# Mean squares of the second attention's norm: one float32 matmul, or two float32r matmuls of the squares' high and low parts

## The chip, the cores and the metric

The kernel runs on one core of a Trainium2 chip. A core has a matrix engine (TensorE, PE), whose weight loads have a column of their own in the profile (PEld), a vector engine (VectorE, DVE), a scalar engine (ScalarE, ACT), a general engine (GpSimd, POOL) and an engine that issues most transfers (SyncE, SP). Each engine works through its own list of instructions in order, and semaphores between the lists hold an instruction until its operands are there. The metric is the device time of one execution in microseconds (us), less is better; the times given are medians of several runs.

## The reference

The program is a trunk of two layers on 1024 rows of 1024 float32 values. Layer 0 mixes tokens by latent attention, layer 1 by differential attention; each mixer is followed by its output projection, a layer norm with the residual, a SwiGLU feed-forward part (2816 wide) and another layer norm. The change is in the mixer of layer 1 alone. Cut to it:

```python
def _rmsnorm(x, g):
    y = x32 * lax.rsqrt(jnp.mean(jnp.square(x32), axis=-1, keepdims=True) + RMS_EPS)
    return (y * g.astype(jnp.float32)).astype(x.dtype)

def _diff_mixer(x, w_in, ..., g_sub, w_o, lambda_init):
    q, k, v = jnp.split(x @ w_in, ...)        # 8 heads, 2 maps of 64, values of 128
    ...                                       # for each block of 128 query rows:
        p = jax.nn.softmax(logits, axis=-1)   # scores * scale - slope * distance, chunk mask
        a = p[:, 0] - lam * p[:, 1]
        o = jnp.einsum('bhqk,bkhe->bqhe', a.astype(v.dtype), v, ...)
    o = _rmsnorm(o, g_sub) * (1.0 - lambda_init)    # over the 128 values of a head
    return o.reshape(b, s, DIFF_HEADS * DIFF_V) @ w_o
```

For every head and row the norm needs the mean of 128 squares.

## The kernel before, in words

Products of float32 matrices are made of three matmuls of type float32r: each operand is split into a high part (a cast to float32r) and a low part (what the cast left off), and high x high, high x low and low x high are summed in PSUM. The helper `split` (L486, L487) makes the parts, with the cast on ACT and the subtraction on another engine, most often DVE. Only a few matmuls take float32 operands as they are; the one for the mean squares is among them.

The second attention runs from about 1135 to 1575 us. `attention` goes through pairs (head h, block i of 128 query rows), eight blocks to a head; the last head goes in the order 6, 7, 4, 5, 2, 3, 0, 1. For each pair there are three steps, with the scores two blocks ahead of the transposes:

- `score_b`: for both softmax maps the scores go into a PSUM bank `s_b` (matmuls, L228). DVE adds the bias, moves them into an SBUF tile `l_b` and takes the extreme of each row (L231). ACT makes the exponential in place (L234), POOL scales the second map (L1306) and DVE joins the two (L1307).
- `turn_b`: TensorE transposes the joined map into PSUM `pt_b` (L160); ACT casts it to the high part `pth_b` (L255), DVE subtracts the low part `ptl_b` (L256).
- `mix_b`: for a group g of two blocks, TensorE multiplies by the values (`o_b`, L267), and DVE copies the result into `bo`, which has the 128 values of the head on the partitions and the query rows along the columns (L1316).

Between these, numbered slots hold other work: `proj_b` makes queries and keys of the next head (PSUM `bp`, L155 to L157, three float32r matmuls per term), `values_b` the values (`bv`). `norm_b` and `norm_b2` of head h stand at the slots 8h+9 and 8h+10, in the next head's run. `norm_b` squares `bo` on ACT into `sq`. `norm_b2` multiplies by `ones` (a 128 x 128 matrix of 1/128) on TensorE into an `s` bank `ms`, so that each column's mean stands on all partitions. Then ACT takes logarithm (L1340) and exponential with -0.5 (L1342), and POOL multiplies `bo` by the result (L1343). Heads 0 to 5 are then written out to DRAM (L1346). Heads 0 to 6 are normed in two parts of 512 columns; the last head in groups: `sq7_3` and `sq7_2` of 256 columns, `sq7_0` of 512. Of 17 such parts 15 have 512 columns.

`l_b` and `sq` come from one ring, tag "l" of pool `lp`, with five buffers of 4 KB per partition. PSUM has three `s` banks.

In the last head `begin_out` frees the memory of `xT` (the input of `proj_b`), loads the output weights `wo` there (L358), and the rows of heads 0 to 5 come back as `of_a` (L371). The output projection splits rows into `oh_a` (ACT L394, DVE L395) and multiplies by `wo` (`zp_a`, L406).

The order of each engine's list is set by a scheduler that runs over the program with a simulated timeline when the kernel is built, and by priorities for some steps. A shorter or longer instruction thus can move others.

Of the kernel before, what the change touches and what calls it, by code (L numbers as in the profile page):

```python
# [9 lines left out]
F32 = mybir.dt.float32  # L10
F32R = mybir.dt.float32r
# [5 lines left out]
P = 128  # L17
S = 1024
# [24 lines left out]
def trunk(  # L43
# [33 lines left out]
    V, A, G, T = nc.vector, nc.scalar, nc.gpsimd, nc.tensor  # L77

    cp = ctx.enter_context(tc.tile_pool(name="cp", bufs=1))
    sp = ctx.enter_context(tc.tile_pool(name="sp", bufs=8))  # L80

    ident = cp.tile([P, P], F32, tag="ident", name="ident")
    ones = cp.tile([P, P], F32, tag="ones", name="ones")
    cst = cp.tile([P, 48], F32, tag="cst", name="cst")
    edge = ctx.enter_context(tc.tile_pool(name="edge", bufs=1, side="right"))
    late = edge.tile([P, 504], F32, tag="edge", name="edge")
    wp = ctx.enter_context(tc.tile_pool(name="wp", bufs=3))
    big = ctx.enter_context(tc.tile_pool(name="big", bufs=5))
    ps, ps_bufs, ps_stack = None, None, None
# [10 lines left out]
    dr = ctx.enter_context(tc.tile_pool(name="dr", bufs=1, space=DRAM))  # L100

    V.memset(ones, 1.0 / P)
    mhalf = cst[:, 0:2]
    V.memset(mhalf, -0.5)
    eps_rms = cst[:, 8:9]
# [2 lines left out]
    def f32(t):  # L108
        return t.bitcast(F32)
# [4 lines left out]
    def ps_s(name):  # L114
        return ps.tile([P, 512], F32, tag="s", bufs=ps_bufs[0], name=name)
# [225 lines left out]
    class OutProj:  # L341
# [50 lines left out]
        def split(self, tb, hs, o):  # L392
            oh, ol = (t[:, hs] for t in self.oh[tb])
            A.activation(oh, o, AF.Copy, scale=self.scale)  # L394
            V.scalar_tensor_tensor(ol, o, self.scale, f32(oh), ALU.mult, ALU.subtract)  # L395
# [674 lines left out]
    with ast as st:  # L1070
        pool = st.enter_context(tc.tile_pool(name="a1", bufs=2, reuse_waits="tile"))
        vp = st.enter_context(tc.tile_pool(name="a1v", bufs=12, side="right", reuse_waits="tile"))
        lp = st.enter_context(tc.tile_pool(name="a1l", bufs=4, side="right", reuse_waits="tile"))
# [155 lines left out]
    with ExitStack() as st:  # L1229
        lp = st.enter_context(tc.tile_pool(name="b1l", bufs=5, reuse_waits="tile"))  # L1230
# [4 lines left out]
        vt, lt, pts, sqs, q_slot = {}, {}, {}, {}, {}  # L1235
# [82 lines left out]
        def o_rows(h, g, n=1):  # L1318

            return ob[:, h % 2, g * 256:(g + n) * 256]  # L1320
# [4 lines left out]
        def norm_b(h, g0=0, g1=4):  # L1325

            t = lp.tile([P, S], F32, tag="l", name=f"sq{h}_{g0}")
            sqs[h, g0] = [(t[:, (g - g0) * 256:min(g + 2, g1) * 256 - g0 * 256],
                           o_rows(h, g, min(2, g1 - g))) for g in range(g0, g1, 2)]
            for sq, o in sqs[h, g0]:  # L1330
                A.activation(sq, o, AF.Square)

        def norm_b2(h, g0=0, g1=4):
            parts = []
            for i, (sq, o) in enumerate(sqs.pop((h, g0))):
                m = ps_s(f"ms{h}_{g0}_{i}")[:, :sq.shape[1]]
                T.matmul(m, ones, sq, start=True, stop=True)
                parts.append((sq, o, m))
            for r, _, m in parts:
                A.activation(r, m, AF.Ln, bias=eps_rms, scale=1.0)  # L1340
            for r, o, _ in parts:
                A.activation(r, r, AF.Exp, scale=-0.5)  # L1342
                G.tensor_tensor(o, o, r, ALU.mult)  # L1343
            if h < H - 2:
                for g in range(g0, g1):
                    nc.sync.dma_start(o_dr[1][g][h], o_rows(h, g))  # L1346
# [36 lines left out]
        for h in range(H - 1):  # L1383
            at(8 * h + 9, norm_b, h)
            at(8 * h + 10, norm_b2, h)
        at(8 * H - 6, norm_b, H - 1, 3, 4)
        at(8 * H - 5, norm_b2, H - 1, 3, 4)
        at(8 * H - 4, norm_b, H - 1, 2, 3)
        at(8 * H - 3, norm_b2, H - 1, 2, 3)

        first, second = LAST_ORDER[:2]
# [111 lines left out]
```

## Time and profile before

| | |
|---|---|
| median of 3 runs | 2294.41 us (2293.27 to 2299.95) |
| the profiled execution | 2294.99 us, its span 2293.2 us, mean granted TensorE clock 0.996 |
| PE, matmuls | 2251.4 us busy, 98% of the span |
| PEld, weight loads | 1918.7 us, 84% |
| DVE | 1560.4 us, 68% |
| ACT | 1018.6 us, 44% |
| POOL | 877.9 us, 38% |
| DMA | 289.33 MB, 126 GB/s |

The busy time of an engine is the time in which at least one of its instructions runs; an instruction's own duration can overlap that of the next, so on TensorE the distance between the starts of successive matmuls tells what each occupies. A row of the timeline has start, duration, engine, line, operation, output<-inputs, shape, count, and in brackets the wait ahead of it with the instruction that ended it. Shares are averages over stages with different limits; the row of a stretch of time tells the limit in that stretch.

### The profile page before, as it was taken

What the parts mean: (1) busy time and instruction counts of PE and PEld (TensorE: products, weight loads), DVE (VectorE), ACT (ScalarE), POOL (GpSimd) and SP (SyncE); (2) the same over time, 40 slices, a digit from 0 to 9 for tenths busy, and PEclk for the clock granted to TensorE, in tenths of its full rate; (3) what the DMA queues carried; (4) which work ended last, traced back from release to release, by engine and by line L of the source; (5) the groups of instructions that cost most, each with busy time, mean ns of one, the idle gap of its engine ahead of it and who ended that gap; (6) DMA issues with size and microseconds to landing.
All of it is one profiled execution on the core that took longest, in us unless ns stands there. A gap on an engine that the chain in (4) does not pass through costs nothing. (4 is left out here: it accounts for less than half of the span.)

```text
span 2293.2 us, 31159 instructions
## 1 busy us (share of the span) xinstructions
PE 2251.4 (98%) x11426; PEld 1918.7 (84%) x11426; DVE 1560.4 (68%) x2887; ACT 1018.6 (44%) x2101; POOL 877.9 (38%) x682
## 2 busy tenths in 40 slices
PE   9999999999999999999999999999999999999997
PEld 9888998888888887888888898977778888887886
DVE  6666665596656558777476766676587566658877
ACT  4465664342332324345455655555442233324353
POOL 2233451124444445555332424211024444436564
PEclk9999999999999999999999999999999999999999
DMA  5121335334323237544311202143344232337453
GB/s 205 41 94 61 117 99 190 142 139 144 108 87 120 93 116 305 200 176 166 104 45 33 69 25 70 38 193 120 124 166 155 70 128 80 127 126 301 144 203 123
DMA packets 104281, 289.33 MB, mean 126 GB/s; under 512 B 8640, under 2 KB 31808, under 8 KB 93632
## 3 DMA queue, kind: packets, MB, share of 16 engines
q1 hardware_dynamic: 100128, 277.90, 34.5%
q0 software_dynamic: 4000, 9.44, 1.4%
q8 instruction: 90, 1.47, 0.3%
q14 instruction: 63, 0.52, 0.1%
HBM read 205.78 MB, written 77.33 MB: 123 GB/s over the span
## 5 line engine op out<-in xcount | busy, mean ns | idle before, releaser
L486 ACT CAST op_g<-gr 128x512 fp32r<-128x512 f32 x240 | 147.5, 622 | 410.8 <-PE gb L531 229.9
L487 POOL TENSOR_TENSOR op_g<-gr,op_g 128x512 fp32r<-128x512 f32 x104 | 145.3, 1402 | 304.1 <-DVE tmp L622 154.0
L487 DVE TENSOR_TENSOR op_h<-rh,op_h 128x512 fp32r<-128x512 f32 x154 | 166.4, 1112 | 68.1 <-ACT op_h L486 68.1
L531 PE MATMUL ga<-xh_m,op_g 128*128 128x512 f32 x512 | 168.1, 389 | 0.0
L486 ACT CAST op_h<-rh 128x512 fp32r<-128x512 f32 x154 | 92.6, 619 | 148.7 <-DMA rh<-h_dr 39.9
L799 PE MATMUL dw<-op_w_t,op_h 128*128 128x512 f32 x660 | 151.5, 390 | 0.3 <-DVE op_h L487 0.3
L799 PEld LDWEIGHTS dw<-op_w_t,op_h 128*128 128x128 f32 x660 | 123.5, 188 | 26.4 <-DVE op_h L487 1.0
L234 ACT ACTIVATE l_b<-l_b,mx_b 128x256 f32<-128x256 f32 (+7 forms) x128 | 99.5, 778 | 75.9 <-DVE mx_b L231 74.0
L1306 POOL TENSOR_SCALAR l_b<-l_b,r_b,cst 128x128 f32<-128x128 f32 (+3 forms) x64 | 52.5, 821 | 207.6 <-DVE r_b L236 201.6
L487 POOL TENSOR_TENSOR op_w_t<-tt,op_w_t 128x512 fp32r<-128x512 f32 x66 | 100.1, 1521 | 80.0 <-ACT op_w_t L486 77.6
L799 PE MATMUL dx<-op_w_b,op_h 128*128 128x512 f32 x528 | 123.5, 394 | 5.4 <-ACT op_w_b L486 3.9
L799 PEld LDWEIGHTS dx<-op_w_b,op_h 128*128 128x128 f32 x528 | 99.8, 190 | 28.7 <-ACT op_w_b L486 4.7
L531 PE MATMUL gb<-t4h_f,op_g 128*128 128x512 f32 x352 | 115.9, 390 | 3.0 <-DVE tmp L614 3.0
L531 PE MATMUL gc<-b22h_f,op_g 128*128 128x512 f32 x352 | 115.6, 389 | 2.3 <-ACT op_g L486 2.3
L531 PE MATMUL gc<-t1h_f,op_g 128*128 128x512 f32 x352 | 115.5, 389 | 0.0
L487 DVE TENSOR_TENSOR op_g<-gr,op_g 128x512 fp32r<-128x512 f32 x136 | 109.5, 806 | 8.8 <-ACT op_g L486 8.2
L531 PE MATMUL gb<-t3h_f,op_g 128*128 128x512 f32 x352 | 115.2, 389 | 0.0
L531 PE MATMUL gb<-t2h_f,op_g 128*128 128x512 f32 x352 | 114.9, 389 | 0.0
L531 PEld LDWEIGHTS ga<-xh_m,op_g 128*128 128x128 f32 x512 | 96.1, 188 | 19.9
L487 POOL TENSOR_TENSOR op_g<-s,op_g 128x512 fp32r<-128x512 f32 x40 | 55.5, 1387 | 144.0 <-ACT op_g L486 144.0
L155 PE MATMUL bp<-xT_f,h_wb 128*128 128x512 f32 x256 | 102.8, 402 | 0.0
L157 PE MATMUL bp<-xT_f,l_wb 128*128 128x512 f32 x256 | 101.6, 397 | 0.0
(373 smaller groups left out, 6767.7 us busy)
## 6 DMA issues: line engine op xcount, KB each, us to landing
gr<-in_w_gu SPq DMA_DIRECT2D x44, 1024.0 KB, 6.8
rh<-h_dr SPq DMA_DIRECT2D x28, 1024.0 KB, 5.2
h_dr<-sh SPq DMA_DIRECT2D x22, 1024.0 KB, 4.9
h_dr<-hp SPq DMA_DIRECT2D x22, 768.0 KB, 4.1
tt<-in_w_dn SPq DMA_DIRECT2D x22, 512.0 KB, 7.6
rh<-h_dr SPq DMA_DIRECT2D x14, 768.0 KB, 4.4
z<-xs_dr SPq DMA_DIRECT2D x16, 512.0 KB, 11.1
rw_b<-in_w_dn SPq DMA_DIRECT2D x8, 1024.0 KB, 8.2
```

The lines of the kernel that those rows point to most:

```text
L155: T.matmul(ps_out, lh, rh, start=(i == 0), stop=False)
L157: T.matmul(ps_out, ll, rh, start=False, stop=(i == n - 1))
L234: newest["exp"] = A.activation(l[:, :n], l[:, :n], AF.Exp, bias=mx, scale=-1.0, accum_out=sm).ins
L486: A.copy(hi, src)
L487: eng.tensor_tensor(lo, src, f32(hi), ALU.subtract)
L531: T.matmul(o, w[:, a, kc], x[b][:, k, :], start=(first and k == 0 and (a, b) == (0, 0)), stop=(k == 3 and a == 1), skip_group_check=True,)
L799: T.matmul(o, h[:, a, c], w[:, b_], start=(first and (a, b_) == (0, 0)), stop=(last and a == 1), skip_group_check=True,)
L1306: G.tensor_scalar(l1[:, :n], l1[:, :n], r1, nlam, ALU.mult, ALU.mult)
```

## The change

`norm_b` splits each part's squares with `split`, the cast on ACT and the subtraction on DVE, into a tile `sp` of the ring "l", which holds the high and the low half. `norm_b2` then makes two float32r matmuls with `ones_r`, a float32r copy of `ones` made once at the start, which sum into the same bank. 1/128 is a power of two, so `ones_r` holds it in full. Room for `ones_r` comes from a tile `late` at the edge of SBUF, which becomes 128 columns narrower. The branch under `if False` isn't taken. Lines below the first edits move by 2, those below `norm_b` by 11.

```diff
--- before.py
+++ after.py
@@ -83,7 +83,8 @@
     ones = cp.tile([P, P], F32, tag="ones", name="ones")
     cst = cp.tile([P, 48], F32, tag="cst", name="cst")
     edge = ctx.enter_context(tc.tile_pool(name="edge", bufs=1, side="right"))
-    late = edge.tile([P, 504], F32, tag="edge", name="edge")
+    late = edge.tile([P, 376], F32, tag="edge", name="edge")
+    ones_r = edge.tile([P, P], F32R, tag="ones_r", name="ones_r")
     wp = ctx.enter_context(tc.tile_pool(name="wp", bufs=3))
     big = ctx.enter_context(tc.tile_pool(name="big", bufs=5))
     ps, ps_bufs, ps_stack = None, None, None
@@ -100,6 +101,7 @@
     dr = ctx.enter_context(tc.tile_pool(name="dr", bufs=1, space=DRAM))
 
     V.memset(ones, 1.0 / P)
+    A.copy(ones_r, ones)
     mhalf = cst[:, 0:2]
     V.memset(mhalf, -0.5)
     eps_rms = cst[:, 8:9]
@@ -1327,14 +1329,23 @@
             t = lp.tile([P, S], F32, tag="l", name=f"sq{h}_{g0}")
             sqs[h, g0] = [(t[:, (g - g0) * 256:min(g + 2, g1) * 256 - g0 * 256],
                            o_rows(h, g, min(2, g1 - g))) for g in range(g0, g1, 2)]
-            for sq, o in sqs[h, g0]:
+            for i, (sq, o) in enumerate(sqs[h, g0]):
                 A.activation(sq, o, AF.Square)
+                nm = f"sp{h}_{g0}_{i}"
+                if False:
+                    u = wp.tile([P, 2, 512], F32R, tag="wr", name=nm, bufs=2)
+                else:
+                    u = lp.tile([P, S], F32R, tag="l", name=nm).rearrange("p (a c) -> p a c", a=2)
+                u = [u[:, j, :sq.shape[1]] for j in range(2)]
+                split(u, sq, V)
+                sqs[h, g0][i] = (sq, o, u)
 
         def norm_b2(h, g0=0, g1=4):
             parts = []
-            for i, (sq, o) in enumerate(sqs.pop((h, g0))):
+            for i, (sq, o, u) in enumerate(sqs.pop((h, g0))):
                 m = ps_s(f"ms{h}_{g0}_{i}")[:, :sq.shape[1]]
-                T.matmul(m, ones, sq, start=True, stop=True)
+                for j in range(2):
+                    T.matmul(m, ones_r, u[j], start=(j == 0), stop=(j == 1))
                 parts.append((sq, o, m))
             for r, _, m in parts:
                 A.activation(r, m, AF.Ln, bias=eps_rms, scale=1.0)
```

In heads 0 to 6 TensorE's neighbours of the matmuls stay. Here are head 1's in TensorE's list, between the terms of a projection (`bp`, with `xT` and weights `h_wb`, `l_wb`) and the next scores (`s_b`), before:

```order
L156 MATMUL bp3_0_0_12061<-xT10_f0_10049,h_wb3_0_12057 128x512
L157 MATMUL bp3_0_0_12061<-xT00_f0_10048,l_wb3_0_12058 128x512
L1337 MATMUL ms1_0_0_12092<-sq1_0_11971,ones_62 128x512
L1337 MATMUL ms1_0_1_12094<-sq1_0_11971,ones_62 128x512
L155 MATMUL bp3_0_1_12147<-xT01_f0_10050,h_wb3_0_12057 128x512
L228 MATMUL s_b2_5_0_0_12107<-bk0_10189,bq1_10188 128x384
```

and after:

```order
L158 MATMUL bp3_0_0_12077<-xT10_f0_10051,h_wb3_0_12073 128x512
L159 MATMUL bp3_0_0_12077<-xT00_f0_10050,l_wb3_0_12074 128x512
L1348 MATMUL ms1_0_0_12108<-sp1_0_0_11983,ones_r_68 128x512 x2
L1348 MATMUL ms1_0_1_12111<-sp1_0_1_11987,ones_r_68 128x512 x2
L157 MATMUL bp3_0_1_12165<-xT01_f0_10052,h_wb3_0_12073 128x512
L230 MATMUL s_b2_5_0_0_12125<-bk0_10191,bq1_10190 128x384
```

Each of the two matmuls became two with another operand; the neighbours stayed.

In the last head, the order changes. TensorE's list around `ms7_3`, the mean squares of group 3 (rows of blocks 6 and 7), before (`zp_a` is the output projection, `pt_b` a transposed map):

```order
L228 MATMUL s_b7_3_1_0_15468<-bk1_10190,bq0_10187 128x512
L1337 MATMUL ms7_3_0_15493<-sq7_3_15441,ones_62 128x256
L228 MATMUL s_b7_3_1_0_15468<-bk1_10190,bq1_10188 128x512
L406 MATMUL zp_a1_7_1_0_15564<-wo1_5_15142,oh_a1_7_15126 128x512
L228 MATMUL s_b7_0_0_0_15519<-bk1_10190,bq0_10187 128x128
L228 MATMUL s_b7_0_0_0_15519<-bk1_10190,bq1_10188 128x128
L267 MATMUL o_b7_2_15498<-pth_b7_4_0_15417,bvh3_0_13933 128x256
```

and after:

```order
L162 MATMUL pt_b7_2_0_15602<-ident_61,l_b7_2_0_15446 128x128 x3
L1348 MATMUL ms7_3_0_15554<-sp7_3_0_15501,ones_r_68 128x256
L230 MATMUL s_b7_0_0_0_15581<-bk1_10192,bq0_10189 128x128
L230 MATMUL s_b7_0_0_0_15581<-bk1_10192,bq1_10190 128x128
L269 MATMUL o_b7_2_15560<-pth_b7_4_1_15477,bvh3_2_14453 128x256
L1348 MATMUL ms7_3_0_15554<-sp7_3_0_15501,ones_r_68 128x256
```

The matmul for `sq7_3` stood inside the second score pair of block 3; now its two halves stand behind three transposes of block 2, with two scores of block 0 and a value product between them. The score pair of `s_b7_3_1` and `zp_a` have moved ahead of six more value products (`o_b7_2`), which end just ahead of the transposes.

ACT's list at the same place, before (`L1340` and `L1342` are logarithm and exponential of the norm, `L234` the exponential of scores):

```order
L234 ACTIVATE l_b7_3_0_15457,sm_b7_3_0_15463<-l_b7_3_0_15457,mx_b7_3_0_0_15461 128x512
L1340 ACTIVATE sq7_3_15441<-ms7_3_0_15493,cst_63 128x256
L255 CAST pth_b7_4_1_15421<-pt_b7_5_0_15479 128x2x128
L1342 ACTIVATE sq7_3_15441<-sq7_3_15441 128x256
L234 ACTIVATE l_b7_3_1_15467,sm_b7_3_1_15473<-l_b7_3_1_15467,mx_b7_3_1_0_15471 128x512
L255 CAST pth_b7_2_0_15544<-pt_b7_2_0_15540 128x2x128
```

and after:

```order
L236 ACTIVATE l_b7_3_0_15518,sm_b7_3_0_15524<-l_b7_3_0_15518,mx_b7_3_0_0_15522 128x512
L257 CAST pth_b7_2_0_15606<-pt_b7_2_0_15602 128x2x128
L1351 ACTIVATE sq7_3_15499<-ms7_3_0_15554,cst_63 128x256
L1353 ACTIVATE sq7_3_15499<-sq7_3_15499 128x256
L236 ACTIVATE l_b7_3_1_15528,sm_b7_3_1_15534<-l_b7_3_1_15528,mx_b7_3_1_0_15532 128x512
L257 CAST pth_b7_2_1_15610<-pt_b7_2_0_15602 128x128
```

Logarithm and exponential of `sq7_3` stand ahead of the exponential of `l_b7_3_1` in both; the cast of `pth_b7_4_1`, which stood between the two, went ahead of all these rows, and that of `pth_b7_2_0` (L255, now L257) now stands ahead of them instead of behind.

DVE's list at the end of the last head, before (`z_a` is the residual, L414 adds the projection to it):

```order
L236 RECIPROCAL r_b7_1_1_15592<-sm_b7_1_1_15590 128x1
L414 SCALAR_TENSOR_TENSOR z_a1_6_15121,sum_a1_6_15123<-z_a1_6_15121,zp_a1_6_0_6_15657 128x512
L414 SCALAR_TENSOR_TENSOR z_a1_6_15121,sum_a1_6_15123<-z_a1_6_15121,zp_a1_6_1_6_15665 128x512
L1316 COPY bo_10191<-o_b7_1_15630 128x256
L395 SCALAR_TENSOR_TENSOR oh_a1_4_15773<-bo_10191,cst_63,oh_a1_4_15773 128x256
L1307 SCALAR_TENSOR_TENSOR l_b7_1_0_15574<-l_b7_1_0_15574,r_b7_1_0_15582,l_b7_1_1_15584 128x256
L395 SCALAR_TENSOR_TENSOR oh_a1_5_15864<-bo_10191,cst_63,oh_a1_5_15864 128x256
```

and after, in two pieces. The first stands some rows earlier, where before the list went from L231 of `l_b7_1_0` straight to L256:

```order
L233 ISA l_b7_1_0_15639,mx_b7_1_0_0_15643<-s_b7_1_0_0_15640,bb_10187 128x256
L233 ISA mx_b7_1_0_0_15643 128x1
L489 TENSOR_TENSOR sp7_2_0_15616<-sq7_2_15614,sp7_2_0_15616 128x256
L258 TENSOR_TENSOR ptl_b7_2_0_15607<-pt_b7_3_0_15661,pth_b7_2_0_15606 128x2x128
L1309 SCALAR_TENSOR_TENSOR l_b7_0_0_15580<-l_b7_0_0_15580,r_b7_0_0_15588,l_b7_0_1_15590 128x128
```

The second answers to the rows shown of before:

```order
L238 RECIPROCAL r_b7_1_1_15657<-sm_b7_1_1_15655 128x1
L416 SCALAR_TENSOR_TENSOR z_a1_6_15171,sum_a1_6_15173<-z_a1_6_15171,zp_a1_6_0_6_15723 128x512
L416 SCALAR_TENSOR_TENSOR z_a1_6_15171,sum_a1_6_15173<-z_a1_6_15171,zp_a1_6_1_6_15731 128x512
L1318 COPY bo_10193<-o_b7_1_15696 128x256
L258 TENSOR_TENSOR ptl_b7_0_0_15713<-pt_b7_0_0_15710,pth_b7_0_0_15712 128x128
L1309 SCALAR_TENSOR_TENSOR l_b7_1_0_15639<-l_b7_1_0_15639,r_b7_1_0_15647,l_b7_1_1_15649 128x256
```

The new subtraction for `sp7_2` stands ahead of the scores `l_b7_1_1`, and the split of `oh_a1_4` (L395, now L397) no longer stands ahead of the joining of `l_b7_1_0` (L1307, now L1309).

## The prediction

> **What bounds the kernel now.** I read the page's busy shares first, then busy time by stretch over the second attention (1135 to 1575 us, the only part the change touches), then the new tiles' relatives, the waits of TensorE there, and last the timeline around single places.
>
> ```profile
> PE 2251.4 (98%) x11426; PEld 1918.7 (84%) x11426; DVE 1560.4 (68%) x2887; ACT 1018.6 (44%) x2101; POOL 877.9 (38%) x682
> ```
> ```profile
> 1300.00:1355.00 55.00, 55.00 (x362) 50.00 (x361) 36.78 (x110) 30.54 (x74) 16.02 (x16) 1.00 0.14 39
> 1355.00:1410.00 55.00, 55.00 (x325) 48.45 (x324) 36.05 (x109) 33.68 (x75) 21.14 (x18) 1.00 0.19 58
> 1465.00:1520.00 55.00, 50.89 (x275) 43.32 (x275) 34.07 (x92) 27.57 (x55) 14.10 (x14) 0.94 0.43 158
> 1520.00:1575.00 55.00, 52.41 (x280) 43.93 (x279) 40.99 (x114) 30.55 (x77) 12.68 (x14) 0.97 0.34 119
> ```
> The columns of the stretches are length, then busy us of PE, PEld, DVE, ACT and POOL, the granted clock, DMA. In the heads that still have projections to interleave, TensorE is busy for the whole 55 us, while VectorE (DVE) is idle for 18 and ScalarE (ACT) for 21 to 24. Of these only the last two show TensorE idle. So a TensorE instruction that gets shorter there is worth its length, and work on DVE and ACT has room, as long as no wait reaches TensorE. What it waits for between 1135 and 1620 us, on the matmul side:
>
> ```profile
> PE zp_a L406 <- DMA wo<-wo_dr: 3.7, 1, 3.7
> PE pt_b L160 <- DVE l_b L1307: 3.3, 2, 2.2
> ```
> That is nearly all of it: one load of output weights, and two waits for scaled scores.
>
> **What is removed and added on TensorE.**
>
> ```profile
> L1337 PE MATMUL ms<-sq,ones x34: 379/592/645, 1202.5 to 1568.8; 128*128 128x512 f32 x30, 128*128 128x256 f32 x4
> ```
> 34 records for 17 instructions: each float32 matmul goes through the array as two records, 15 instructions with 512 columns and 2 with 256. Durations overlap, so I price by starts.
>
> ```profile
> 1302.66 1.02 PE L1337 MATMUL ms<-sq,ones 128*128 128x512 f32 x2
> 1303.12 0.79 PE L155 MATMUL bp<-xT_f,h_wb 128*128 128x512 f32 x1
> 1303.75 0.39 PE L156 MATMUL bp<-xT_f,h_wb 128*128 128x512 f32 x1
> ...
> 1305.07 0.40 PE L155 MATMUL bp<-xT_f,h_wb 128*128 128x512 f32 x1
> 1305.30 0.39 PE L156 MATMUL bp<-xT_f,h_wb 128*128 128x512 f32 x1
> ```
> A float32r matmul of 512 columns takes 1305.30 - 1305.07 = 0.23 us of the array. From the start of `ms` to the start of the second matmul behind it are 1.09 us; less the one L155 between, the float32 `ms` takes 0.86 us. Two float32r matmuls take 0.46, so each saves 0.40.
>
> ```profile
> 1546.13 0.59 PE L1337 MATMUL ms<-sq,ones 128*128 128x256 f32 x2
> 1546.38 0.58 PE L228 MATMUL s_b<-bk,bq 128*128 128x512 f32 x1
> 1546.80 0.39 PE L406 MATMUL zp_a<-wo,oh_a 128*128 128x512 f32 x1
> ...
> ```
> The same for 256 columns, where the L406 row is the next start: 0.67 - 0.23 = 0.44.
>
> ```profile
> 1547.36 0.28 PE L267 MATMUL o_b<-ptl_b,bvh 128*128 128x256 f32 x1
> 1547.48 0.28 PE L267 MATMUL o_b<-pth_b,bvl 128*128 128x256 f32 x1
> ```
> Float32r of 256 columns: 0.12, two 0.24, saving 0.20. Sum: 15 x 0.40 + 2 x 0.20 = 6.4 us, all on the bound engine. The 17 added weight loads are behind matmuls: PEld has 5 to 7 us free in each 55 us.
>
> **What is added on ACT and DVE.**
>
> ```profile
> L486 ACT CAST op_g<-gr 128x512 fp32r<-128x512 f32 x240 | 147.5, 622 | 410.8 <-PE gb L531 229.9
> L487 DVE TENSOR_TENSOR op_g<-gr,op_g 128x512 fp32r<-128x512 f32 x136 | 109.5, 806 | 8.8 <-ACT op_g L486 8.2
> L487 DVE TENSOR_TENSOR op_h<-rh,op_h 128x512 fp32r<-128x512 f32 x154 | 166.4, 1112 | 68.1 <-ACT op_h L486 68.1
> L255 ACT CAST pth_b<-pt_b 128x256 fp32r<-128x256 f32 x128 | 45.1, 368 | 32.8 <-PE pt_b L160 22.4 <-DVE ptl_b L256 9.5
> L1261 DVE TENSOR_TENSOR bvl<-bv,bvh 128x256 fp32r<-128x256 f32 x24 | 10.1, 420 | 5.4 <-ACT bvh L1260 5.2
> ```
> The split is the helper that the feed-forward part uses, so the first three rows are the same instructions on the same shapes: a cast of 0.62 us and a subtraction of 0.81 (1.11 in the group with the busier POOL; I take 0.81 and keep 1.11 as the end). 256 columns are about 0.37 and 0.42. Sum: ACT 15 x 0.62 + 2 x 0.37 = 10 us, DVE 15 x 0.81 + 2 x 0.42 = 13 us (to 18), over 370 us in which ACT is idle for 40% and DVE for a third. In heads 0 to 6 the projections, which stand between the norm's instructions on TensorE, hide this: `ms` stands some 20 us of TensorE work behind the scores that precede the squares. I cost it at nothing there; if that cover were gone, 1.4 us per part would come to light (0.62 + 0.81), more than the 0.40 saved. No DMA is added, and SP's and POOL's instructions only change places with neighbours.
>
> `ones_r` is one cast of 128 columns, first on ACT.
>
> ```profile
> 3.03 0.40 ACT L961 CAST xh<-x 128x256 fp32r<-128x256 f32 x1 [1.02 <-DMA x<-in_xt]
> ```
> The cast fits in ACT's 1.02 us of waiting for the first input (a cast of twice its columns takes 0.40): nothing, but should it not fit, 0.3 us.
>
> **The load of output weights.** Could the 3.7 us wait swallow the gain, because the load comes no earlier?
>
> ```profile
> 1500.39 0.39 PE L157 MATMUL bp<-xT_f,l_wb 128*128 128x512 f32 x1
> ...
> 1510.38 2.05 PE L406 MATMUL zp_a<-wo,oh_a 128*128 128x512 f32 x4 [3.67 <-DMA wo<-wo_dr]
> ```
> ```profile
> 1500.81 0.96 SPq L371 DMA_DIRECT2D of_a<-o_dr  x2
> 1501.82 2.95 SPq L358 DMA_DIRECT2D wo<-wo_dr  x6
> ```
> The loads are issued right after TensorE's last reading of `xT` (1500.39 plus 0.39), whose memory they fill. They move with TensorE, and the work between them and the wait stands as before. The wait stays, the gain passes.
>
> **The tail.** In the last head there are no projections, and the order around `ms7_3` changes. Before, the matmul for `sq7_3` stands inside the second score pair of block 3. Now its low half ends behind seven value products, three transposes, two small scores and its own two matmuls: 9 x 0.12 + 3 x 0.22 (0.86 x 128 / 512) + 2 x 0.06 (half of 0.12) = 1.8 us after that pair.
>
> ```profile
> 1547.13 0.47 ACT L1340 ACTIVATE sq<-ms,cst 128x256 f32<-128x256 f32 x1
> ...
> 1547.74 0.44 ACT L1342 ACTIVATE sq<-sq 128x256 f32<-128x256 f32 x1
> 1548.13 0.72 ACT L234 ACTIVATE l_b<-l_b,mx_b 128x512 f32<-128x512 f32 x1
> ```
> The first two rows are the logarithm and the exponential of `sq7_3`, the third is the exponential of the scores `l_b7_3_1`, which in the new order still stands behind both. The score pair ends on TensorE at about 1546.6 (1546.38 + 0.23). With 1.8 us more, 0.47 and 0.44, and 0.14 for the handover (from 1559.26, the end of the L1307 below, to its transpose at 1559.40), it starts at 1549.45, not 1548.13: 1.3 us later. Behind it on ACT stand the splits of the output rows and the square and the new cast for `sq7_2`; on DVE the new subtraction `sp7_2` stands ahead of the scores `l_b7_1_1`; and TensorE waits for that chain already:
>
> ```profile
> 1558.38 0.48 DVE L395 SCALAR_TENSOR_TENSOR oh_a<-bo,cst,oh_a 128x256 fp32r<-128x256 f32 x1
> 1558.78 0.48 DVE L1307 SCALAR_TENSOR_TENSOR l_b<-l_b,r_b,l_b 128x256 f32<-128x256 f32 x1
> ```
> ```profile
> 1559.40 0.41 PE L160 MATMUL pt_b<-ident,l_b 128*128 128x128 f32 x2 [2.22 <-DVE l_b L1307]
> ```
> So I add 1.3 us. Its bounds are -2.2 (the wait goes) and +2.1 (1.3, a cast of 0.37 and a subtraction of 0.42 all pass through). I take 1.3 because the added subtraction takes the place of the split in the L395 row (0.48), which the new order puts behind the awaited instruction, and ACT's exponential of `sq7_2` (0.44, as that of `sq7_3`) moves behind the scores' in exchange for the cast.
>
> A wait of TensorE also costs what follows it:
>
> ```profile
> 1557.00:1559.40 2.40, 0.18 (x2) 0.07 (x2) 2.40 (x8) 0.80 (x2) 0.55 (x1) 1.00 0.10 29
> 1559.40:1562.00 2.60, 2.60 (x8) 2.09 (x9) 1.25 (x5) 1.79 (x5) 0.00 (x0) 0.59 0.01 3
> 1562.00:1565.00 3.00, 3.00 (x15) 2.67 (x14) 2.65 (x6) 0.63 (x1) 0.56 (x1) 0.79 0.04 8
> 1230.00:1231.20 1.20, 0.13 (x1) 0.00 (x0) 1.20 (x2) 0.10 (x2) 0.00 (x0) 1.00 0.00 0
> 1231.20:1234.00 2.80, 2.76 (x19) 2.42 (x20) 2.36 (x11) 2.12 (x8) 0.45 (x1) 1.00 0.00 0
> ```
> After the wait of 2.4 us the clock was 0.59 and 0.79 for 5.6 us: 0.41 x 2.6 + 0.21 x 3.0 = 1.7 us more. After the wait of 1.2 us it stayed 1.00. The Trainium skill ("TensorE: Matmul & The Clock Gate", section "What's actually happening") has the clock halve after an idle window of about 3.4 us; by that rule the 2.2 us wait would cost 2.2 alone. The trace disagrees, or its window counts something else; by the row the wait is worth 3.9, and the row decides.
>
> **Sum.** -6.4 + 1.3 = -5.1 us. The profiled execution took 2294.99 us (span 2293.2), 0.58 over the median of the runs, 2294.41, so either gives the same difference: 2294.41 - 5.1 = 2289.3 us, -0.22%. About 0.3% (6.9 us) is what a measurement of this kernel can tell from no change (its three runs spread over 6.7 us), so I expect a real gain that mostly stays below that.
>
> **Rivals.**
> *The tail's wait goes as well.* For it: the new order takes the exponential of `sq7_2` from ahead of the scores' exponential on ACT. Against it: the 1.3 us above. Then -6.4 - 2.2 - 1.7: 2284.1 us.
> *The gain is swallowed before 1510 us*, by the weight load or by waits that refill. Then only the five matmuls after it count, 3 x 0.40 + 2 x 0.20 = 1.6, less the tail's 1.3: 2294.1 us. The rows at 1500 us speak against it.
> *Slower: the ring of score tiles.* A split tile occupies one of the five `l` buffers, two per head, beside the squares' one, from cast to `ms`; two are left for scores, of which each block needs two while the one before is still to be transposed. A score's reduction then waits on DVE, its PSUM bank is held, and TensorE, in order, stands at the next score. For it: five buffers were just enough. Against it: DVE had 18 us free in 55, and in the new order 20 us of projections stand there. With one wait per head like that at 1230 us (1.1), 7 x 1.1 = 7.7: 2294.41 - 6.4 + 7.7 = 2295.7. With one like that at 1557 us (3.9 with its slow clock), 27.3: 2315. The gain is gone at 0.9 us per head, and slower by 0.3% begins at 13.3 / 7 = 1.9.
>
> **Chances.** My forecast (2286.5 to 2292.5) 0.52; the tail's wait gone 0.17; swallowed 0.16; ring 0.15, half of it beyond 2301.3. Faster by over 0.3% (below 2287.5): 0.17 and a fifth of the forecast's 0.52, 0.28. Slower by over 0.3%: 0.07. Within: 0.65. The range from 2284.0 (the first rival) to 2296.0 (the ring's cheap form) leaves out some 0.1 above and a little below.
>
> **What would show it.** Right: 34 `ms` matmuls of float32r with 0.23 us between starts; TensorE still busy for all of the stretches from 1250 to 1465 us; the last `bp` matmul some 5 us earlier than 1500.39 (12 x 0.40 before it); 3.7 us for `wo` as now; a wait of `pt_b` for L1309 (the old L1307) of 2 to 4 us near 1553. Wrong: waits of `s_b`, `pt_b` or `ms` in heads 1 to 6, DVE's L233 (the old L231) waiting for `ms` or `pt_b`, a subtraction far over 1.1 us, or `ms` on the chip at 0.4 us per matmul.

## The result: 0.4% slower

The changed kernel took 2303.70 us (median of 6 runs, 2303.18 to 2306.25), the kernel before 2295.42 in the same comparison. The ratio is 1.0038 with a 95% interval of 1.0029 to 1.0048: 8.3 us slower, where 5.1 us faster was forecast. The profiled execution took 2303.26 us, its span 2301.2.

The busy shares of the profile after show nothing of it, TensorE stays at 98%:

```profile
PE 2250.1 (98%) x11426; PEld 1920.6 (83%) x11426; DVE 1578.0 (69%) x2904; ACT 1026.0 (45%) x2119; POOL 875.6 (38%) x682
```

The stretches of the second attention do. Columns as in the prediction: length, busy us of PE, PEld, DVE, ACT, POOL, granted clock, DMA.

```profile
1190.00:1245.00 55.00, 50.42 (x319) 45.21 (x318) 42.10 (x121) 34.15 (x84) 15.62 (x15) 0.94 0.12 34
1245.00:1300.00 55.00, 55.00 (x344) 49.76 (x343) 34.61 (x101) 30.33 (x69) 20.67 (x17) 1.00 0.20 59
1300.00:1355.00 55.00, 52.98 (x333) 47.32 (x332) 40.26 (x116) 32.74 (x79) 17.30 (x17) 1.00 0.15 39
1355.00:1410.00 55.00, 55.00 (x343) 49.81 (x342) 35.51 (x104) 32.28 (x72) 20.64 (x17) 1.00 0.20 58
1410.00:1465.00 55.00, 53.25 (x325) 47.86 (x324) 39.77 (x115) 32.07 (x76) 16.65 (x16) 0.97 0.15 39
```

Every second stretch has holes on TensorE now, those of heads 1, 3 and 5; the others are full, as before (1.1 us of head 1's 4.6 was idle before too). TensorE's waits, matmul side, over 1135 to 1640 us:

```profile
PE s_b L230 <- DVE mx_b L233: 5.4, 6, 1.2
PE zp_a L408 <- DMA wo<-wo_dr: 4.6, 1, 4.6
PE pt_b L162 <- DVE nmu_a L180: 1.9, 1, 1.9
PE pt_b L162 <- DVE l_b L1309: 1.8, 2, 0.9
PE o_b L269 <- DVE ptl_b L258: 1.5, 2, 0.7
```

The first row is new: scores wait for DVE's reduction of earlier ones, which has to free their bank.

To see where the time goes I matched the same matmuls in two profiles and took the start in one minus that in before's. The table gives the median over 8 us behind the time in its head (times of before's profile, us), for the kernels told of below, one execution of each (not before_6 and after_6, which changed more). Heads 1 to 6 lie between the columns 1190 and 1495, the last head and the output projection between 1495 and 1636, the start of the feed-forward part between 1636 and 1700. The first column differs by what the executions' beginnings differed in, so differences between columns count; before_q4, which should differ from before in nothing that costs time, moves by 1.4 us between them.

```
                1190    1248    1495    1636    1700
after           -0.5     5.7     8.7     8.9     8.7
hold            -1.5     4.0     9.8    11.6    13.2
odd             -1.5    -1.5    -4.2    -3.5    -3.7
high_only       -0.7    -1.8    -7.6    -6.7    -3.3
bf16            -0.3     2.6     6.7     6.8     8.1
pt_ring         -1.6    -2.3     0.8     0.7     4.6
before_wv       -3.4     0.1     0.1    -1.1    -1.0
after_wv        -1.4     4.2     3.2     3.8     3.7
before_q4       -0.8     0.0     0.5     0.6     0.4
after_q4        -0.2     2.7    -0.5     0.8     0.8
hold_q4         -2.2     1.0     1.7     2.4     2.2
pt_ring_q4      -1.3    -1.9    -6.0    -7.0    -3.6
mix_q4          -3.3    -3.9    -7.9    -8.2    -8.2
```

The changed kernel lost 9.2 us in heads 1 to 6, where 12 shorter `ms` should have given 4.8: something there costs 14 us. The last head is nearly neutral (0.2 us lost).

**What happens in head 1.** The mean squares of head 0 and the first scores of block 5 (384 columns) on TensorE, before:

```profile
1203.89 1.02 PE L1337 MATMUL ms<-sq,ones 128*128 128x512 f32 x2
1207.04 0.51 PE L228 MATMUL s_b<-bk,bq 128*128 128x384 f32 x2
```

and after, with the matmul behind the first part's `ms`:

```profile
1203.67 0.63 PE L1348 MATMUL ms<-sp,ones_r 128*128 128x512 f32 x2
1204.15 0.39 PE L159 MATMUL bp<-xT_f,l_wb 128*128 128x512 f32 x1
...
1207.91 0.63 PE L1348 MATMUL ms<-sp,ones_r 128*128 128x512 f32 x2
1208.49 0.51 PE L230 MATMUL s_b<-bk,bq 128*128 128x384 f32 x2
```

The pair of matmuls occupies 1204.15 - 1203.67 = 0.48 us, as costed. But the second part's `ms` stands 4.0 us later, and the scores of block 5 right behind it. In the built program the two maps of block 5 got the buffers of `sp0_0_0` and `sp0_0_1`: they can't begin before `ms` has read those. Before, they got buffers of block 3. In head 3 the same scores came 8.5 us later than before (1316.78, not 1308.25).

A few us later that meets something else. DVE's joining of block 5's two maps (768 columns) and POOL's next instruction, before:

```profile
1215.18 1.02 DVE L1307 SCALAR_TENSOR_TENSOR l_b<-l_b,r_b,l_b 128x768 f32<-128x768 f32 x1 [0.67 <-POOL l_b L1306]
1217.20 2.40 POOL L147 TENSOR_TENSOR l_wb<-r_wb,h_wb 128x1024 fp32r<-128x1024 f32 x1 [2.05 <-ACT h_wb L146]
```

and after, with the reduction behind it on DVE and what TensorE waited for:

```profile
1216.58 2.39 POOL L149 TENSOR_TENSOR l_wb<-r_wb,h_wb 128x1024 fp32r<-128x1024 f32 x1
1216.64 3.15 DVE L1309 SCALAR_TENSOR_TENSOR l_b<-l_b,r_b,l_b 128x768 f32<-128x768 f32 x1 [0.67 <-POOL l_b L1308]
1219.71 0.67 DVE L233 CUSTOM_DVE_ANT_0 l_b<-s_b,bb,mx_b 128x448 f32<-128x448 f32 x1
1219.94 0.85 PE L162 MATMUL pt_b<-ident,l_b 128*128 128x128 f32 x6 [0.90 <-DVE l_b L1309]
1222.40 0.50 PE L230 MATMUL s_b<-bk,bq 128*128 128x512 f32 x1 [1.15 <-DVE mx_b L233]
```

POOL's subtraction for the weights of the next head (`l_wb`) used to start after the joining had ended. In both, the joining waits for POOL's scaling of the same maps. Now, 1.5 us later, the high part of the weights is there by then, and POOL goes on with them at once: both start together, and the joining takes 3.15 us instead of 1.02. I call this a collision. The same happens in heads 3 and 5, at block 6 (3.28 us each instead of 1.14). Behind it on DVE the reductions of scores wait, and TensorE for them. At the end of the head its other work runs out: no projection and no product for the values starts between 1226.5 and 1242.8 us, where before that gap was 1228.7 to 1236.0. A slow clock follows:

```profile
1230.60:1235.00 4.40, 1.88 (x8) 1.08 (x8) 3.25 (x14) 2.73 (x9) 1.37 (x2) 0.82 0.00 0
1235.00:1240.00 5.00, 5.00 (x21) 4.70 (x20) 4.29 (x19) 4.20 (x14) 0.85 (x2) 0.50 0.00 0
1240.00:1246.00 6.00, 6.00 (x50) 5.80 (x49) 4.07 (x13) 4.10 (x12) 1.00 (x2) 0.98 0.00 0
```

### The profile page after: what moved, and what is told of

It reads as the page before. It is cut to its first block, busy times and chain, and to the rows that moved or that the text cites. A ratio compares the mean times of both kernels' runs of the same rounds, so it can differ in the third digit from the quotient of the medians.

```text
span 2301.2 us, 31200 instructions
## 1 busy us (share of the span) xinstructions
PE 2250.1 (98%) x11426; PEld 1920.6 (83%) x11426; DVE 1578.0 (69%) x2904; ACT 1026.0 (45%) x2119; POOL 875.6 (38%) x682
```

## Experiments

Three explanations are weighed. Ring (or lateness) theory: the tiles that the change holds make later scores wait for their buffers, so these come late. Work theory: the 17 casts and subtractions delay the chain of the attention. Collision theory: the joinings that run beside POOL's subtraction for the weights are the price.

Times are medians; the ratio is to the kernel before, on the same chip (2294.8 to 2296.2 us), with its 95% interval. The edits are shown by their main lines; "..." marks what is left out.

| kernel | us | ratio |
|---|---|---|
| hold | 2308.61 | 1.0065 (1.0052 to 1.0078) |
| odd | 2294.01 | 0.9996 (0.9987 to 1.0005) |
| high_only | 2293.17 | 0.9992 (0.9983 to 1.0001) |
| bf16 | 2309.14 | 1.0056 (1.0044 to 1.0069) |
| before_6 | 2327.71 | 1.0137 (1.0124 to 1.0151) |
| after_6 | 2333.51 | 1.0168 (1.0154 to 1.0182) |
| before_wv | 2297.73 | 1.0007 (0.9998 to 1.0015) |
| after_wv | 2297.07 | 1.0006 (0.9997 to 1.0015) |
| pt_ring | 2300.52 | 1.0023 (1.0014 to 1.0032) |
| after_q4 | 2295.55 | 0.9997 (0.9988 to 1.0006) |
| before_q4 | 2295.43 | 0.9998 (0.9989 to 1.0007) |
| pt_ring_q4 | 2292.69 | 0.9989 (0.9981 to 0.9998) |
| mix_q4 | 2289.72 | 0.9975 (0.9966 to 0.9985) |
| hold_q4 | 2298.56 | 1.0015 (1.0006 to 1.0023) |

### The held buffers alone, and the work without them

hold, on the kernel before:

```diff
+            G.memset(t[:, :1], 0.0)
+            for i, (sq, o) in enumerate(sqs[h, g0]):
+                u = lp.tile([P, S], F32, tag="l", name=f"sp{h}_{g0}_{i}")[:, :sq.shape[1]]
+                A.activation(u, o, AF.Square)
+                sqs[h, g0][i] = (sq, o, u)
...
-                T.matmul(m, ones, sq, start=True, stop=True)
+                T.matmul(m, ones, u, start=True, stop=True)
```

> The kernel before with the change's buffers and nothing else of it: the squares go straight into two `sp` tiles of the ring of score tiles, beside the one `sq` tile as now (touched by a one-column memset on POOL), so a head's norm holds three of the five buffers until its `ms` matmuls, which stay float32. No cast, no subtraction, no float32r. Ring theory (the held buffers tie the scores of block 5 to the `ms` matmuls, in heads 1, 3 and 5): slower than before by 7 to 15 us, since the changed kernel lost 8.3 us although its matmuls gave some 6.4 back; 2302 to 2310. Work theory (the 17 casts and subtractions on ACT and DVE delay the chain): as before, 2295.4, within 2 us. Collision theory (the price is DVE's joining of two maps beside POOL's weight split): slow only if L1307 again shows rows of over 3 us beside POOL's L147; about 3 us for each.

2308.61 us, 13.6 slower than before. No cast, no subtraction, no new matmul: the held buffers are enough to lose more than the change did. The work theory falls. The collisions, one each in heads 1, 3 and 5, are there too, and the waits behind them. POOL, DVE and TensorE in head 3:

```profile
1338.16 2.40 POOL L147 TENSOR_TENSOR l_wb<-r_wb,h_wb 128x1024 fp32r<-128x1024 f32 x1
1338.23 3.40 DVE L1307 SCALAR_TENSOR_TENSOR l_b<-l_b,r_b,l_b 128x1024 f32<-128x1024 f32 x1 [1.14 <-POOL l_b L1306]
1343.46 0.45 PE L228 MATMUL s_b<-bk,bq 128*128 128x384 f32 x1 [1.41 <-DVE mx_b L231]
```

and the first of TensorE's waits from 1190 to 1460 us:

```profile
PE s_b L228 <- DVE mx_b L231: 5.6, 5, 1.4
```

odd takes the new path only in odd heads (`norm_b2` makes the float32 matmul where there is no split):

```diff
             for i, (sq, o) in enumerate(sqs[h, g0]):
                 A.activation(sq, o, AF.Square)
+                if not (h % 2 == 1):
+                    sqs[h, g0][i] = (sq, o, None)
+                    continue
...
```

> The change for heads 1, 3, 5 and 7 only; heads 0, 2, 4 and 6 keep one float32 matmul and one ring tile. The norms of heads 1, 3 and 5 stand among the blocks of heads 2, 4 and 6, where the changed kernel's trace gained; those of 0, 2 and 4 stand where it lost 4 to 6 us each. Ring theory: the losing places are as before, so 7 parts x 0.40 + 2 x 0.20 = 3.2 us faster than before, 2292. Work theory: half of the work, half of the loss: 2299 to 2300.

2294.01, 1.0 faster, not told from no change by its interval; the table has 2.7 us gained in heads 1 to 6, where 6 x 0.40 = 2.4 was due. With the even heads' norm as it was, the loss is gone: it comes from the norms that stand in heads 1, 3 and 5. This run has collisions too, of 3.00 us each at block 4 of heads 3 and 5 (0.88 alone), and lost nothing by them in this sum.

high_only has one float32r matmul per part, and squares written as float32r:

```diff
-            t = lp.tile([P, S], F32, tag="l", name=f"sq{h}_{g0}")
+            t = lp.tile([P, S], F32R, tag="l", name=f"sq{h}_{g0}")
...
-                for j in range(2):
-                    T.matmul(m, ones_r, u[j], start=(j == 0), stop=(j == 1))
+                T.matmul(m, ones_r, u[0], start=True, stop=True)
```

> One float32r matmul per part on the squares rounded to float32r by the instruction that squares; the low part is left out, and the two steps after it (logarithm, exponential) write float32r into the same tile. No cast, no subtraction, one ring tile per head as before. Both theories: nothing holds the saving back, so 15 x (0.86 - 0.23) + 2 x (0.44 - 0.12) = 10.1 us faster than before, 2285. If a shorter `ms` is worth nothing on the path: 2295.

2293.17, only 1.8 faster: a miss for all theories. By the table it was 6.9 us ahead at 1495 (12 x 0.63 = 7.6 were due), and lost 3.4 again between 1636 and 1700. More of that below. Collisions are in it as well, three of 3.0 to 3.7 us in heads 2, 3 and 5, one of them here (DVE and POOL, head 3). What heads 1 to 6 lack, 7.6 - 6.9 = 0.7 us, is all that they can have cost together:

```profile
1305.83 3.02 DVE L1309 SCALAR_TENSOR_TENSOR l_b<-l_b,r_b,l_b 128x640 f32<-128x640 f32 x1 [1.09 <-POOL l_b L1308]
1305.77 2.40 POOL L149 TENSOR_TENSOR l_wb<-r_wb,h_wb 128x1024 fp32r<-128x1024 f32 x1
```

bf16 puts both parts' halves into one ring tile:

```diff
+            v = lp.tile([P, 2 * S], mybir.dt.bfloat16, tag="l", name=f"sp{h}_{g0}").rearrange("p (i a c) -> p i a c", i=2, a=2)
...
+                A.copy(u[0], sq)
+                V.tensor_tensor(u[1], sq, u[0], ALU.subtract)
```

> The change with high and low parts in bfloat16 (and `ones` in bfloat16), so that both parts of a head fit in one ring tile: two tiles held per head, where the change holds three and before holds one; the same casts, subtractions and pairs of matmuls. Ring theory: part of the loss goes, 2290 to 2300. Work theory: all of it stays, 2302 to 2305.

2309.14, no better than the change. Two tiles held are too many already: the table shows the loss in the same place (7.0 us up to 1495). That the loss would shrink with the number of tiles was wrong. Its profiled execution was the fastest of five (2303.5), so that the table shows less than the median.

### More buffers, and the weights' subtractions elsewhere

before_6 and after_6 change two pools; before_wv and after_wv one argument:

```diff
-        lp = st.enter_context(tc.tile_pool(name="b1l", bufs=5, reuse_waits="tile"))
+        lp = st.enter_context(tc.tile_pool(name="b1l", bufs=6, reuse_waits="tile"))
...
-            vh = pool.tile([P, 256], F32R, tag="vh", name=f"bvh{pr}_{tb}", bufs=10)
+            vh = pool.tile([P, 256], F32R, tag="vh", name=f"bvh{pr}_{tb}", bufs=8)
...
```
```diff
-                wts[which, h] = load_w(w_b_qk[h, which], 1024, f"wb{h}_{which}")
+                wts[which, h] = load_w(w_b_qk[h, which], 1024, f"wb{h}_{which}", eng=V)
```

> The kernel before with six score buffers instead of five; the room comes from the value tiles `vh` and `vl`, eight buffers each instead of ten. It is the measure for the next run. Ring theory: the five were enough for before, so no gain from the sixth; fewer value tiles can cost something: 2293 to 2300.

> The changed kernel with the same six score and eight value buffers. Ring theory: with the sixth buffer the scores of block 5 no longer have to wait for `ms`, so the loss of 8.3 us turns into a gain of 3 to 6 us against the run before_6. Work theory (casts and subtractions delay the chain, whatever the buffers): 6 to 10 us slower than before_6.

2327.71 and 2333.51. The fewer value tiles cost 31 us by themselves, with waits of transposes up to 5.1 us, so the pair is another kernel with other gaps, and its difference of 5.8 us says nothing sure on the ring. Inconclusive.

> The kernel before with the low parts of the query and key weights (the twelve subtractions of 1024 columns on POOL, L147) made on DVE instead, so that nothing of POOL's can run beside DVE's joining of two maps for more than 1.3 us. It is the measure for the next run; DVE gets some 20 us more: 2293 to 2305.

> The changed kernel with the same subtractions on DVE. Its order still has the scores of block 5 behind the `ms` matmuls. Collision theory (three overlaps with POOL's weight split, in which the joining took 3.2 us instead of 1.1, are the price): faster than before_wv by 3 to 6 us. Lateness theory (the scores come late because they need the held buffers, and the collisions only add to it): still slower than before_wv, by 3 to 8 us.

2297.73 and 2297.07: the loss of 8.3 us is gone, with the order of scores still late, and neither theory's number came. By the table the change costs 4.6 - 3.5 + 4.8 = 5.9 us in heads 1 to 6 here, not 14.0. That speaks for the collisions in heads 1, 3 and 5 as most of the price, though the gain stayed at 0.7, and DVE had other work in both. The expectation overlooked that the subtraction for the value weights (`l_wbv`) stays on POOL: after_wv has two collisions with it, of 3.20 and 5.32 us (1.02 alone), in heads 2 and 4.

### The two causes apart, and together

pt_ring takes the halves from the ring of the transposed maps; q4 cuts POOL's subtraction of query and key weights into four:

```diff
-                    u = lp.tile([P, S], F32R, tag="l", name=nm).rearrange("p (a c) -> p a c", a=2)
+                    u = [ptp.tile([P, 2, 256], F32R, tag=f"pt{c}", name=f"{nm}{c}").rearrange("p a c -> p (a c)")
+                         for c in "hl"]
...
```
```diff
-        j = (eng or G).tensor_tensor(lo[:, :cols], raw[:, :cols], f32(hi[:, :cols]), ALU.subtract)
+        n = 256 if name.startswith("wb") and not name.startswith("wbv") else cols
+        for c in range(0, cols, n):
+            j = (eng or G).tensor_tensor(
+                lo[:, c:c + n], raw[:, c:c + n], f32(hi[:, c:c + n]), ALU.subtract)
```

> The change with the high and low parts in the ring of the transposed maps (`pth` and `ptl`, four buffers each of just this size) instead of the ring of score tiles; the same casts, subtractions and matmuls. Ring theory: head 1's scores of block 5 are back where they were (the program's order shows it), those of heads 3 and 5 still stand late, so part of the loss goes: 2293 to 2299. Work theory: the loss stays, 2302 to 2305.

> The changed kernel with the twelve subtractions for the query and key weights' low parts still on POOL, but each in four instructions of 256 columns instead of one of 1024. The scores of block 5 stay behind the `ms` matmuls. Collision theory (the joining on DVE makes no headway until the POOL instruction beside it, 2.4 us, has ended): the joinings of 3.2 us become shorter than 2.0, and the loss against before_q4 falls from 8.3 us to under 3. Lateness theory: the loss against before_q4 stays at 6 to 9.

> The kernel before with the same four pieces: the measure for after_q4. It has no such collision to lose, and 36 more instructions on POOL, which is idle for most of the time: 2294 to 2297.

> Both at once: parts in the ring of the transposed maps, and POOL's subtractions in four pieces. By both theories the best of these: 2289 to 2293 if each removes its share of the loss, that is 3 to 6 us faster than before_q4.

| us | POOL's subtraction whole | in four pieces |
|---|---|---|
| before | 2294.83 | 2295.43 |
| parts in the ring of scores (the change) | 2303.70 (before: 2295.42) | 2295.55 |
| parts in the ring of transposed maps | 2300.52 | 2292.69 |

Both remedies together give a gain, and neither alone does. The pieces take the change from 8.3 us behind to level; they are worth nothing to the kernel before, which had no collision in heads 1 to 6 to lose. The ring alone gives less than was expected by time: 2300.52 lies between the two forecasts, and its interval overlaps a little with that of the change. By the table it takes the cost in heads 1 to 6 from 14.0 to 2.4 + 4.8 = 7.2 us, and 3.9 us more go behind 1636, of which more below. In after_q4 the joining of head 1 is back at 1.02 us, because the pieces run ahead of POOL's scaling, and the one of head 3 (block 7) that still meets them takes 1.85 (POOL and DVE of either place):

```profile
1215.81 2.84 POOL L151 TENSOR_TENSOR l_wb<-r_wb,h_wb 128x256 fp32r<-128x256 f32 x4 [4.24 <-ACT h_wb L148]
1219.66 1.02 DVE L1312 SCALAR_TENSOR_TENSOR l_b<-l_b,r_b,l_b 128x768 f32<-128x768 f32 x1 [0.17 <-POOL l_b L1311]
...
1336.63 3.80 POOL L151 TENSOR_TENSOR l_wb<-r_wb,h_wb 128x256 fp32r<-128x256 f32 x4
...
1336.60 1.85 DVE L1312 SCALAR_TENSOR_TENSOR l_b<-l_b,r_b,l_b 128x1024 f32<-128x1024 f32 x1 [0.47 <-POOL l_b L1311]
```

With both, heads 1 to 6 gain 4.7 us of the 4.8 due, and the profile is 5.7 us further ahead at 1636 than at 1190. Then 3.4 of it go, as in high_only and pt_ring. TensorE at the start of the feed-forward part, in pt_ring_q4, the matmul that waits:

```profile
1664.83 0.66 PE L536 MATMUL gc<-b22h_f,op_g 128*128 128x512 f32 x1 [3.33 <-ACT op_g L491]
```

and the stretches around it:

```profile
1661.00:1665.00 4.00, 0.67 (x4) 0.25 (x3) 4.00 (x8) 3.42 (x8) 0.00 (x0) 1.00 0.00 0
1665.00:1669.00 4.00, 4.00 (x11) 2.94 (x12) 4.00 (x7) 1.93 (x4) 0.00 (x0) 0.57 0.63 264
```

A wait for the split of the gates is there in before too, 2.3 us. Here it is 3.33, and 4 us at a clock of 0.57 follow. TensorE's list ahead of that matmul is the same as in the next run, mix_q4; it is ACT's and DVE's lists, which make the split, that the scheduler wrote otherwise (ACT's first cast of `t2h_f`, ahead of the split, waits 4.92 us for DVE's `xr_m`, 3.51 in mix_q4). The order at 1660 us hung on an edit at 1200 to 1570. Two runs tested that, and the buffers with smaller collisions. mix_q4 is pt_ring_q4 with the last head's parts in the ring of scores, as in the change; hold_q4 is hold with the four pieces (its joinings of block 7 in heads 3 and 5 take 1.7 us, 3.4 in hold).

```diff
-                if False:
-                    u = wp.tile([P, 2, 512], F32R, tag="wr", name=nm, bufs=2)
+                if h < H - 1:
+                    u = [ptp.tile([P, 2, 256], F32R, tag=f"pt{c}", name=f"{nm}{c}").rearrange("p a c -> p (a c)")
+                         for c in "hl"]
                 else:
...
```

> As pt_ring_q4 (parts in the ring of the transposed maps, POOL's weight subtractions in four pieces), but the last head's parts stay in the ring of score tiles as in the change. By the program's order the feed-forward part of layer 1 then begins as in the kernel before. pt_ring_q4 was 7.0 us ahead at 1640 us and gave 3.6 back by 1690 us, where a wait for ACT's split of the gates stood in a new place. If that order is what took it back: 5 to 7 us faster than before_q4, 2288.5 to 2290.5. If the gain is lost there whatever the order: 2292 to 2294.

> The run hold (the change's three held buffers, float32 matmuls, no split) with POOL's weight subtractions in four pieces. Lateness and overlaps both count: 4 to 8 us slower than before_q4 (the 6.4 us that the change saved on TensorE and that after_q4 did not show, 2300 to 2303), against 13.6 with whole pieces. If the overlaps are all there is: 2295 to 2297. If the pieces do nothing here: 2306 to 2310.

mix_q4 took 2289.72 us, 5.2 faster than before (2294.91) and the fastest of all; its interval lies wholly below 1, and overlaps a little with that of pt_ring_q4. The wait at the feed-forward part is as before:

```profile
1661.90 0.50 PE L536 MATMUL gc<-b22h_f,op_g 128*128 128x512 f32 x1 [2.39 <-ACT op_g L491]
```

The stretch behind it has the full clock:

```profile
1662.00:1666.00 4.00, 4.00 (x18) 3.18 (x19) 4.00 (x7) 2.02 (x5) 0.00 (x0) 1.00 0.62 262
```

And TensorE's waits from 1190 to 1460 us are down to these:

```profile
PE pt_b L165 <- DVE l_b L1312: 1.1, 1, 1.1
PE s_b L233 <- DVE mx_b L236: 0.2, 1, 0.2
```

Yet mix_q4 has collisions. Block 5's joinings in heads 2 and 4 took 3.73 and 3.74 us, beside the subtraction for the value weights, which is still whole (head 2, DVE, then POOL):

```profile
1263.60 3.73 DVE L1312 SCALAR_TENSOR_TENSOR l_b<-l_b,r_b,l_b 128x768 f32<-128x768 f32 x1 [0.77 <-POOL l_b L1311]
...
1263.52 0.56 POOL L1290 DMA_DIRECT2D bq<-bq  x1
1264.11 2.40 POOL L151 TENSOR_TENSOR l_wbv<-r_wbv,h_wbv 128x1024 fp32r<-128x1024 f32 x1
```

Neither before nor the change has these. before_q4 and pt_ring_q4 have them too, and in none of the three did heads 2 and 4 lose time. So a collision isn't a price by itself, as odd and high_only showed: those that cost stood in heads 1, 3 and 5, in kernels whose norm there holds more tiles than before. Why those places cost and others don't, no run shows further.

hold_q4 took 2298.56, 3.7 slower than before and 3.1 slower than before_q4 (expected 4 to 8). So of the 13.6 us of hold, lateness by itself is about 3, and the collisions with what follows them about 10. By the table: 3.9 of 11.3 in heads 1 to 6. For the change itself, by the table: the cost in heads 1 to 6 fell from 14.0 us to 4.8 - 0.3 = 4.5 in after_q4, of which 2.9 + 0.8 = 3.7 fall in head 1, whose joining of block 5 collides no longer. This split is a difference of runs, and the pieces also move other instructions. In hold and hold_q4 the scores of block 5 keep their places in TensorE's list; in after_q4 those of heads 3 and 5 stand about half as late as in the change, so some of what it got back there may be lateness.

## Why the prediction was wrong

The saving on TensorE was right. The pair of matmuls took 0.48 us against 0.46 costed, and where nothing stands in the way heads 1 to 6 give 4.6 to 4.7 us of 4.8 (mix_q4, pt_ring_q4). mix_q4's 2289.7 is within half a microsecond of the time that the prediction gave to the change, in part by the luck of the tail, below. The load of `wo` stayed a wait (4.6 us, 3.7 before). The tail: 0.2 us lost between 1495 and 1636 where five shorter `ms` should give 1.6, so 1.8 us of loss against 1.3 forecast. That these are close is luck: the wait for the joining, 2.2 us before, was to grow by 1.3 and was 1.9 (the third of TensorE's waits after; the profile names the DVE instruction behind the joining). Waits of 0.8 for `s_b` and 0.4 for `ms`, new there, and 0.9 more for `wo` came in its place. The 17 added weight loads of the prediction don't exist: the float32 matmuls had two each as well, 34 before and after. The casts cost what was put for them, the subtractions less:

```profile
L488 ACT CAST sp<-sq x17: 389/623/633, 1196.6 to 1579.2; 128x512 fp32r<-128x512 f32 x15, 128x256 fp32r<-128x256 f32 x2
L489 DVE TENSOR_TENSOR sp<-sq,sp x17: 426/685/729, 1197.4 to 1580.1; 128x512 fp32r<-128x512 f32 x15, 128x256 fp32r<-128x256 f32 x2
```

A cast is 0.62 as taken, a subtraction 0.69, not 0.81.

The step that failed is the price of nothing for what the norm adds in heads 0 to 6: "I cost it at nothing there", because "the projections, which stand between the norm's instructions on TensorE, hide this". The projections did hide the casts and subtractions: mix_q4 makes all of them and gains 4.6 of the 4.8 us due. They did not hide the held buffers, which cost 14 us in heads 1 to 6. The rival of the ring named that mechanism, and the waits of `s_b` in heads 1 to 6, named as the sign against the forecast, are the first row of the waits after. It was given 0.15, and three things in its weighing were wrong.

- Its counter-argument, 20 us of projections, fits `ms1`, whose list is shown. That TensorE's neighbours stay in heads 0 to 6 is not so: at `ms0`, `ms2` and `ms4` the second part's matmuls had moved back and the scores of block 5 stood right behind them. These norms stand in heads 1, 3 and 5, the losing ones.
- It was priced as a wait in each of seven heads, 1.1 or 3.9 us. It was 14 us in three heads. A wait for a buffer hardly shows as one: the scheduler knew of the buffers and had written the scores late, with projections in between. The price fell due some 10 to 25 us later, towards the head's end, in waits for other things.
- The largest part, up to 14.0 - 4.5 = 9.5 us by the pieces, was in no term: the collisions that late scores led to. The row with 1.11 us against 0.81 ("the group with the busier POOL") was in the prediction, and only the small end was taken from it, as the price of the new subtraction. That an old instruction, L1307, could move into a 2.4 us POOL instruction was not asked.

The Trainium skill states the rule that was missing ("SBUF — State Buffer", section "Who interferes with whom"): a DVE instruction with two inputs in SBUF contends with a GpSimd instruction that reads SBUF, for ports that are locked to one of them, and the order of issue decides which one waits. The trace agrees: POOL's started 0.06 us ahead of the joining and ended at 1218.97, the joining at 1219.79, 0.82 us later, where it takes 1.02 alone.

## What to carry to other kernels

A buffer is a resource like an engine: before adding a tile to a ring, find who gets that buffer next and where the scheduler then puts it, at every place where the step recurs, not at one. When an edit moves work by a microsecond or two, look at what DVE and POOL will do at the same time, and where TensorE's waits follow a collision, try cutting the long POOL instruction into pieces; not every collision costs, as heads 2 and 4 of mix_q4 show. Read the gain where it is made, and then follow it to the end: a changed order elsewhere can take it back, as at the feed-forward part.

## What the runs showed of the hardware

A DVE instruction that has lost to POOL does not always get its turn when that one POOL instruction ends. In head 1 of the changed kernel it did. In bf16 (and in pt_ring alike) the joining of 640 columns, 0.88 us alone, took 4.33, through four POOL instructions, two of which only issue transfers (DVE, then POOL):

```profile
1313.79 4.33 DVE L1309 SCALAR_TENSOR_TENSOR l_b<-l_b,r_b,l_b 128x640 f32<-128x640 f32 x1 [0.31 <-POOL l_b L1308]
...
1313.71 0.58 POOL L1287 DMA_DIRECT2D bq<-bq  x1
1314.32 1.30 POOL L1351 TENSOR_TENSOR bo<-bo,sq 128x512 f32<-128x512 f32 x1
1315.56 0.57 POOL L1287 DMA_DIRECT2D bq<-bq  x1
1316.15 1.27 POOL L1351 TENSOR_TENSOR bo<-bo,sq 128x512 f32<-128x512 f32 x1
```

In after_q4 it did get in between four pieces (1.85 us, while POOL's four took 3.80 instead of 2.84). There the joining had started 0.03 us ahead of the first piece, but that isn't the whole reason: in hold_q4 one of 1024 columns started 0.12 us behind it (1335.25 and 1335.13) and took 1.70, where 1.28 is its time alone. In mix_q4, as in bf16, the joining got no turn between the issue of a transfer and the instruction behind it. What decides stays open.

The clock after a single wait: full after 2.39 us (mix_q4), 0.57 over the next 4 us after 3.33 us (pt_ring_q4), at the same place of the program. That fits the window of about 3.4 us in the Trainium skill ("TensorE: Matmul & The Clock Gate", section "What's actually happening") better than the tail of before did, where 0.59 followed a wait of 2.2; and several short waits, 2.5 us in 4.4, brought 0.50 in head 1 of the changed kernel. One wait's length does not settle it.
